# An encoder layer: where the first three weight slots of the projections are loaded and split

## The chip, the cores and the metric

The kernel runs on one core of one Trainium2 chip. The time is device microseconds of the whole program, from one execution to the next the median of several. The engines are PE (matrix products), PEld (PE's weight loads), DVE (vector), ACT (scalar), POOL (GpSimd) and SP, which issues all DMAs of this kernel.

## The reference

One layer of a hybrid encoder on two groups of 512 rows (here: prompt and sample), D = 1024, all in float32. Cut to what matters here:

```python
def _swiglu(x, w_gu, w_down):
    gate, up = jnp.split(x @ w_gu, 2, axis=-1)
    return (jax.nn.silu(gate) * up) @ w_down

def _layer(x, mem, p):
    x = _layernorm(ALPHA * x + 0.5 * _swiglu(x, p['ffn1_wgu'], p['ffn1_wd']), p['ln1_g'], p['ln1_b'])
    h = x @ p['w_in']
    br_a = _mla(h[..., :OFF_KV], h[..., OFF_KV:OFF_RWKV], ...) @ p['p_mla']
    br_b = _rwkv7(h[..., OFF_RWKV:OFF_GATE], ...) @ p['p_rwkv']
    gates = jax.nn.sigmoid(h[..., OFF_GATE:] + p['b_gate']).reshape(b, s, N_BRANCH, D_MODEL)
    mix = (gates[:, :, 0] * br_a + gates[:, :, 1] * br_b) @ p['w_o']
    x = _layernorm(ALPHA * x + mix, p['ln2_g'], p['ln2_b'])
    x = _layernorm(ALPHA * x + _cross(x, mem, ...), p['ln3_g'], p['ln3_b'])
    x = _layernorm(ALPHA * x + 0.5 * _swiglu(x, p['ffn2_wgu'], p['ffn2_wd']), p['ln4_g'], p['ln4_b'])
```

The change lies between the first `_layernorm` and `h = x @ w_in`.

## The kernel before

**Numbers in two parts.** Every float32 operand of a product is split into a high part (a rounding cast, ACT, line 246) and a low part (the operand minus its high part, a subtraction on DVE, line 180, or for x on POOL, line 247). A product is three matmuls: high times high, high times low, low times high (`Bank.prod`). In the profile `whl` is a weight slot's two parts, `wraw` the slot as loaded, `xh` and `xl` the parts of x, `ps` a PSUM bank.

**Weight slots.** A slot is 128 x 1024 numbers (512 KB). `Stream.fetch` takes a raw buffer and a split buffer, issues the load on SP, and writes the cast and the subtraction. The stream `st` feeds everything behind the first feed-forward block; of every four of its slots three use a pool with three split buffers and two raw ones, and the fourth a split buffer of its own with a raw one of that pool. The feed-forward block's weights (`FfnWeights`) use the same buffers, so slots 0 to 2 of `st` take over from the block's last weights.

**First feed-forward block.** `ffn` computes both groups together by Strassen's scheme with seven products (`strassen`), named "1" to "7". The down projection runs in 15 steps (`DOWN`, `down_step`); the last one has m = 3, four pairs, and takes the products in the order 1, 2, 6, 5, 3, 7, 4 (`AT_LAST`). The function `ahead` of a step is called before each of its seven products, with the product's place. Additions on DVE follow the products as their operands appear (`todo`).

**First LayerNorm.** When the last step's sums of a group are there, its x is transposed on PE into banks and DVE takes the statistics (`BlockNorm.add`, `BlockNorm.stats`); the shift `ln_h` is the last of them. Then eight tiles of x are normalised (`Norm.applying`): two DVE instructions, an activation on ACT, a cast on ACT and the low part on POOL. The first group's first three tiles are written ahead of the second group's statistics, the others behind them. `stats` with `hold` sets `k.after`: from then on every DVE instruction that the program writes gets an order behind that shift (class `Held`), until line 1041 sets `k.after = None`.

**Projections.** `compressed(2, "kv_norm_g", decay)` takes slots 0, 1 and 2 and multiplies them with x of one group, then the other, x tile by x tile over three banks at once (`abreast`); `compressed(3, "q_norm_g")` does so with slots 3, 4 and 5. Four banks carry the tag "a". A slot is fetched when the program asks for it:

```python
    def next_slot(self):
        while len(self.ready) <= self.ahead and self.n < len(self.slots):
            self.fetch()
        return self.ready.pop(0)
```

**What sets the order.** Each engine works its queue strictly as it was laid out beforehand. A planner lays it out: of the instructions whose inputs and buffers are there by its modelled times it takes the one that was written first in the program; orders written by hand (`order`, `Held`) are kept. So where a fetch is written decides how its cast and its subtraction rank among the others.

Of the kernel before, what the change touches and what calls it, by code (L numbers as in the profile page):

```python
# [42 lines left out]
def tiles_of(w, ns, ks):  # L43
# [40 lines left out]
DOWN = ((0, 0, 2), (1, 0, 2), (2, 0, 3), (3, 0, 3), (0, 2, 4), (1, 2, 5), (2, 3, 6), (3, 3, 6), (0, 4, 7), (1, 5, 8),  # L84
        (2, 6, 9), (0, 7, 10), (1, 8, 10), (2, 9, 10), (3, 6, 10))
# [219 lines left out]
def op_tiles(places):  # L305


    def pair(name):
        pool, tag, bufs = places[name]
        return [pool.tile([P, 4, T], F32R, name="xo", tag=tag, bufs=bufs) for _ in range(2)]  # L310

    return pair
# [214 lines left out]
            ra, rb = nxt  # L527


def ffn(k, fw, x32, std, rows_of, op_tile, posts, sums, d_h, d_s, norm_of, applied, last=False):  # L530

# [50 lines left out]
    def down_step(n, u2, u4):  # L584
        m, p0, p1_ = DOWN[n]

        def ahead(i):

            if i == 2 and m == 3:
                while due:  # L590
                    due.pop(0)()
            if i == 2:
                for p in range(p1_, max([p1_, *(b for _, _, b in DOWN[n + 1 : n + 2])])):
                    fetch(p)

        ps, done = {}, set()
        y = {(r, c): x32[:, rows_of[r], 2 * m + c] for r in range(2) for c in range(2)}

        def add(out, name, u):
            nc.vector.scalar_tensor_tensor(out=out, in0=ps[name].t, scalar=SC, in1=u, op0=ALU.mult, op1=ALU.add)  # L600

        final = n == len(DOWN) - 1

        def more(r, c, u):

            eng = nc.vector if final else nc.gpsimd
            eng.tensor_tensor(out=y[r, c], in0=y[r, c], in1=u, op=ALU.add)  # L607

        def to_y(r, c, name, u):
            add(y[r, c], name, y[r, c])  # L610
            if not final:
                more(r, c, u)

        def summed(i, x):

            x.add(m // 2)
            if m == 3 and not last:
                if i == 1:  # L620
                    going.append(applied(rows_of[0], norms[0]))
                    for _ in range(3):
                        next(going[0])
                BlockNorm.stats([x], True)
            elif m == 3 and i == 1:
                BlockNorm.stats(norms, True)

        todo = [
            ("p1", "1", lambda: nc.scalar.activation(out=u2, in_=ps["1"].t, func=AF.Identity, scale=SC)),
            ("c11", ("2", "p1"), lambda: to_y(0, 0, "2", u2)),  # L630
            ("u2", ("6", "c11"), lambda: add(u2, "6", u2)),
            ("u4", ("5", "u2"), lambda: add(u4, "5", u2)),
            ("u3", ("7", "u4"), lambda: add(u2, "7", u2)),
            ("c22", ("7", "u4"), lambda: to_y(1, 1, "7", u4)),
            ("c12", ("3", "u4"), lambda: to_y(0, 1, "3", u4)),
            ("c21", ("4", "u3"), lambda: to_y(1, 0, "4", u2)),
        ]
        if final:
            for name, (r, c, of, u) in {"d11": (0, 0, "p1", u2), "d12": (0, 1, "u4", u4), "d22": (1, 1, "u4", u4),
                                        "d21": (1, 0, "u3", u2)}.items():  # L640
                todo.insert(0, (name, (of,), lambda r=r, c=c, u=u: more(r, c, u)))
            todo = [(a, (*b, "d" + a[1:]) if a[0] == "c" else b, f) for a, b, f in todo]
        if p1_ == NP and m == 3:
            for r, x in enumerate(norms):
                todo.append((f"n{r}", (f"c{r + 1}1", f"c{r + 1}2"), lambda r=r, x=x: summed(r, x)))
        elif p1_ == NP and m == 1:
            due.extend(lambda r=r, x=x: summed(r, x) for r, x in enumerate(norms))
        strassen(k, fw, turn_of(n), ps, done, todo, p1_ - p0,
                 lambda o, i: tuple(slot(OPS.index(o), (p0 + i) % 4)[:, j] for j in range(2)), ahead)


    with posts() as sb:
# [13 lines left out]
        for g in range(G):  # L666
            xp = [std[g].pair(i) for i in range(KT)]
            banks = [Bank(k, "a") for _ in range(4)]
            ws = [[(o[0][:, i * P : i * P + P], o[1][:, i * P : i * P + P]) for i in range(KT)] for o in w]
            if last:  # L670
                abreast(banks, ws, xp)
            for j in range(2):
                pg, pu = banks[2 * j : 2 * j + 2]
                if not last:
                    for b, o in zip((pg, pu), ws[2 * j : 2 * j + 2]):
                        b.prod(b.t, list(zip(o, xp)))
                s = sb.tile([P, 2, T], F32, name="s", tag="s", bufs=2)[:, 0]
                nc.scalar.activation(out=s, in_=pg.t, func=AF.Silu)
                nc.vector.tensor_tensor(out=s, in0=s, in1=pu.t, op=ALU.mult)
                to_h(s, d_s[j][g], sb)  # L680
            if g == 0:
                for name in ("S1", "S2", "S3"):
                    ops[name] = op_tile(name)
                hold = [(0, slice(0, 2), sb.tile([P, 2, T], F32, name="up", tag="up", bufs=1))]
                for i in range(2):
                    t = sb.tile([P, 1, T], F32, name=("p1", "u4")[i], tag=("p1", "u4")[i], bufs=1)
                    hold.append((2, slice(i, i + 1), t))
                for name, a, b, op in (("S1", "A21", "A22", ALU.add), ("S2", None, "A11", ALU.subtract)):
                    for h in hold:
                        sums_of(name, a, b, op, *h)  # L690
# [112 lines left out]
def kernel(  # L803
# [15 lines left out]
    k = Ctx()  # L819
# [4 lines left out]
    def pool(name, side="left", space=None):  # L824
        kw = {} if space is None else {"space": space}
        return tc.tile_pool(name=name, bufs=1, side=side, reuse_waits="tile", **kw)
# [20 lines left out]
    d_h = [scratch(f"d_h_{p}", [P, 7, 2, T]) for p in range(NP)]  # L847
    d_s = [[scratch(f"d_s_{j}_{g}", [P, 2, T]) for g in range(G)] for j in range(2)]
# [46 lines left out]
    st = Stream(nc, plan, nc.vector)  # L895
    st.use(*[(wp, 3, 2)] * 3, (wide, 1, 0))
    k.ps = ctx.enter_context(pool("banks", space=PSUM))
    with ExitStack() as f1:
        fp, xo = f1.enter_context(pool("f1")), f1.enter_context(pool("xo"))
        fw = FfnWeights(k, wf1, [(wp, 3)] * 3 + [(wide, 1)], [(wp, 2)] * 2 + [(wide, 1)], wide)  # L900
        x32 = fp.tile([P, G, KT, T], F32, name="x32")
        xs = []
        for g in range(G):

            a = Acts(xpools[g], "x", 4, KT, "x")
            fw.ahead(1)
            for n in range(KT):
                if g == 0 and n < 2:
                    nc.sync.dma_start(out=x32[:, g, n], in_=x_t[:, g, n])
                elif n % 2 == 0:  # L910
                    nc.sync.dma_start(out=x32[:, g, n : n + 2], in_=x_t[:, g, n : n + 2])
                split(nc, a.hi(n), a.lo(n), x32[:, g, n])
                if (g, n) in ((0, 3), (1, 0)):
                    fw.ahead(1)
            xs.append(a)
        nc.sync.dma_start(out=cc, in_=cst)
        x1, ln = [], []

        def sums1():
            ln.append(f1.enter_context(pool("ln1")))  # L920
            return ln[0]

        def norm1(g):
            return BlockNorm(k, ln[0], lambda n: x32[:, g, n], "ln1_g", "ln1_b", ("c", "bc"[g]))

        def applied1(g, norm):
            def store(m):
                if m % 2:
                    nc.sync.dma_start(out=d_x1[g][:, m - 1 : m + 1], in_=x32[:, g, m - 1 : m + 1])

            if not x1:
                x1.extend(Acts(xpools[i], "x", 4, KT, "x") for i in range(G))
            return norm.applying(x1[g], store)

        places = {n: (xpools[0], "x", 4) for n in ("A11", "A12")}
        places.update({n: (xpools[1], "x", 4) for n in ("A22", "S4")}, **{n: (xo, "xo", 6) for n in ("S1", "S2", "S3")})
        ffn(k, fw, x32, xs, (0, 1), op_tiles(places), lambda: pool("post1"), sums1, d_h, d_s, norm1, applied1)

    def gate_out(n, g, h, t):
        nc.scalar.activation(out=t, in_=h, func=AF.Tanh, scale=0.5, bias=hbg[:, n : n + 1])  # L940
# [5 lines left out]
    with pool("p2") as sb:  # L946
# [172 lines left out]
        with pool("mla") as sm:  # L1119
# [8 lines left out]
            for h in range(HP):  # L1128
# [3 lines left out]
                for g in range(G):  # L1132
# [10 lines left out]
                    m = sb.tile([P, 8], F32, name="kkn", tag="kkn", bufs=2)  # L1143
# [161 lines left out]
    y32 = keep.tile([P, G, KT, T], F32, name="x32")  # L1305
# [147 lines left out]

    places = {n: (mixed, "xs", 8) for n in ("A11", "A12", "A22", "S4")}
    places.update({n: (keep, "xs", 4) for n in ("S1", "S2")}, S3=(of, "xo", 2))
    ffn(k, fw, y32, x3, (1, 0), op_tiles(places), lambda: pool("post2"), sums2, d_h, d_s, norm4, applied4, True)


def softmax(k, sb, s, scale):
# [544 lines left out]
```

## Time and profile before

| | |
|---|---|
| time, median of 3 runs (lowest, highest) | 2775.86 us (2774.26, 2776.49) |
| profiled execution, its own time | 2775.84 us |
| span of the profiled execution | 2774.1 us |
| granted PE clock, mean over the span | 0.963 |
| PE, PEld busy | 2605.6, 2079.9 us |
| DVE, ACT, POOL busy | 2123.8, 1095.9, 699.1 us |

All single times are microseconds from the start of the span. A row of a timeline gives start, length, engine, line, operation, output<-inputs, shape and count, and in brackets the engine's idle time before it and what ended it. A row of the chain of waits gives start, length and piece. The matmul of a 128 x 128 by 128 x 512 tile has a length of about 0.39 us in such rows; they overlap, and the time from one to the next is read from a stretch and its count.

### The profile page before, as it was taken

The numbers are of one execution on the slowest core, as the hardware profiler recorded it, in microseconds if no ns is written. First come the engines' busy times: TensorE is split into PE (matmuls) and PEld (weight loads), VectorE is DVE, ScalarE is ACT, GpSimd is POOL, SyncE is SP. The second block draws the span as 40 slices with busy tenths as digits, with TensorE's granted clock in tenths as the row PEclk, the third lists the DMA queues.
The fourth block names the chain that finished last, engine by engine and source line by source line (L and its number), as shares of the span: only waits on it lengthen the run. The fifth ranks groups of instructions, "written<-read, shape, count | busy, mean of one in ns | idle before, by whom it ended". The sixth has DMA issues, their size and how long they took to land.

```text
span 2774.1 us, 41500 instructions
## 1 busy us (share of the span) xinstructions
PE 2605.6 (94%) x15600; PEld 2079.9 (75%) x15600; DVE 2123.8 (77%) x3749; ACT 1095.9 (40%) x2008; POOL 699.1 (25%) x479
## 2 busy tenths in 40 slices
PE   8999999997899999997989888899999999999996
PEld 7888887785767777776777676677777888887784
DVE  7888887999366777758475768656798888887987
ACT  5334342223353555444443432224554343342222
POOL 0323332443100001133133321103032332332443
PEclk9999999999989999998899898999999999999998
DMA  4344437661244333343434354441101433447751
GB/s 171 130 150 160 152 145 296 235 235 57 95 165 150 112 106 111 111 143 129 131 109 131 119 178 126 161 174 42 54 31 67 161 144 138 152 162 267 273 202 68
DMA packets 164776, 398.18 MB, mean 144 GB/s; under 512 B 41120, under 2 KB 47520, under 8 KB 164576
## 3 DMA queue, kind: packets, MB, share of 16 engines
q1 hardware_dynamic: 164576, 395.53, 40.8%
q8 instruction: 124, 2.03, 0.3%
q14 instruction: 76, 0.62, 0.1%
HBM read 261.50 MB, written 133.96 MB: 143 GB/s over the span
## 4 chain that ended last, share of the span: by engine, by line
PE 76%; DVE 15%; ACT 3%; issue 2%; DMA 2%; POOL 1%; SPq 0%; POOLq 0%; ACTq 0%; DVEq 0%
PE ps L216 73%; PE ps L221 3%; DVE whl L180 2%; DVE dw L180 2%; DVE z L180 1%; DVE x L180 1%; DVE tm L180 1%; DVE rs L180 1%; DVE wt L180 1%; DVE s L180 1%; DVE ln_s L180 1%; DVE phi L180 1%; ACT whl L246 0%; DMA ld<-d_rw 0%; DVE up L180 0%
## 5 line engine op out<-in xcount | busy, mean ns | idle before, releaser
L216 PE MATMUL ps<-xh,whl 128*128 128x512 f32 x2688 | 890.2, 402 | 26.7 <-DVE whl L180 16.8
L216 PE MATMUL ps<-xo,whl 128*128 128x512 f32 x3792 | 899.7, 396 | 14.2 <-DVE z L180 8.5
L216 PEld LDWEIGHTS ps<-xo,whl 128*128 128x128 f32 x3792 | 713.0, 189 | 185.6 <-DVE z L180 6.7
L216 PEld LDWEIGHTS ps<-xh,whl 128*128 128x128 f32 x2688 | 507.8, 190 | 144.2 <-DVE whl L180 20.4
L216 PE MATMUL ps<-xl,whl 128*128 128x512 f32 x1344 | 535.1, 399 | 1.5 <-POOL xl L247 1.5
L180 DVE TENSOR_TENSOR whl<-wraw,whl 128x512 fp32r<-128x512 f32 (+4 forms) x273 | 282.5, 1045 | 63.6 <-ACT whl L246 62.9
L246 ACT CAST whl<-wraw 128x512 fp32r<-128x512 f32 (+4 forms) x318 | 223.9, 715 | 250.1 <-PE ps L216 210.8
L216 PEld LDWEIGHTS ps<-xl,whl 128*128 128x128 f32 x1344 | 255.8, 190 | 55.8 <-POOL xl L247 2.3
L709 POOL TENSOR_TENSOR s<-s,up 128x512 f32<-128x512 f32 x80 | 115.9, 1449 | 626.6 <-DVE up L180 391.1
L246 ACT CAST whl<-wt 128x512 fp32r<-128x512 f32 (+3 forms) x280 | 148.5, 555 | 276.0 <-PE ps L216 164.1
L180 DVE TENSOR_TENSOR whl<-wt,whl 128x512 fp32r<-128x512 f32 (+3 forms) x280 | 216.7, 795 | 10.8 <-ACT whl L246 10.3
L247 POOL TENSOR_TENSOR whl<-wraw,whl 128x1024 fp32r<-128x1024 f32 x45 | 109.1, 2426 | 385.5 <-ACT whl L246 355.4
L246 ACT CAST hop<-s 128x512 fp32r<-128x512 f32 x128 | 79.5, 621 | 238.2 <-POOL s L709 178.0
L180 DVE TENSOR_TENSOR hop<-s,hop 128x512 fp32r<-128x512 f32 x128 | 121.4, 949 | 55.4 <-ACT hop L246 48.0
L180 DVE SCALAR_TENSOR_TENSOR x<-ps,x 128x512 f32<-128x512 f32 x184 | 124.5, 683 | 50.6 <-PE ps L216 50.2
L180 DVE TENSOR_TENSOR wt<-wraw 128x512 f32<-128x512 f32 (+3 forms) x140 | 110.6, 791 | 1.0
L180 DVE TENSOR_TENSOR wt<-wraw,wt 128x512 f32<-128x512 f32 (+3 forms) x140 | 103.1, 737 | 4.2 <-DMA wraw<-in_wf_dram 2.1
L607 POOL TENSOR_TENSOR x<-x,s 128x512 f32<-128x512 f32 x48 | 70.7, 1478 | 129.4 <-DVE x L180 129.4
L247 POOL TENSOR_TENSOR xl<-x,xh 128x512 fp32r<-128x512 f32 x48 | 68.6, 1453 | 91.8 <-ACT xh L246 91.5
L180 DVE TENSOR_TENSOR p<-ps,p 128x512 f32<-128x512 f32 x120 | 82.2, 685 | 7.8 <-PE ps L216 4.8
L607 POOL TENSOR_TENSOR x<-x,z 128x512 f32<-128x512 f32 x48 | 71.3, 1486 | 52.8 <-DVE x L180 49.2
L216 PE MATMUL ps<-mh,whl 128*128 128x512 f32 x256 | 82.2, 401 | 0.0
(328 smaller groups left out, 3728.2 us busy)
## 6 DMA issues: line engine op xcount, KB each, us to landing
d_h<-hop SPq DMA_DIRECT2D x140, 512.0 KB, 2.6
xo<-d_h SPq DMA_DIRECT2D x140, 512.0 KB, 7.2
wraw<-in_wf_dram SPq DMA_DIRECT2D x95, 512.0 KB, 3.4
wraw<-in_wa_dram SPq DMA_DIRECT2D x57, 512.0 KB, 3.5
wraw<-in_wb_dram SPq DMA_DIRECT2D x36, 512.0 KB, 3.4
wraw<-in_wf_dram SPq DMA_DIRECT2D x36, 384.0 KB, 3.9
ld<-d_rw SPq DMA_DIRECT2D x24, 512.0 KB, 4.7
d_gate<-t SPq DMA_DIRECT2D x32, 256.0 KB, 2.4
```

What stands on the lines that cost most here:

```text
L180: inst = f(*args, **kw)
L216: self.last = order(k.tc, k.nc.tensor.matmul(out, a, b, start=start, stop=stop), self.last)
L221: self.last = order(self.k.tc, self.k.nc.tensor.transpose(out, a, ident), self.last)
L246: nc.scalar.copy(hi, src)
L247: (low or nc.vector).tensor_tensor(out=lo, in0=src, in1=hi.bitcast(F32), op=ALU.subtract)
L607: eng.tensor_tensor(out=y[r, c], in0=y[r, c], in1=u, op=ALU.add)
L709: nc.gpsimd.tensor_tensor(out=s[:, i], in0=s[:, i], in1=up[:, i], op=ALU.mult)
```

## The change

`ffn` gets an argument `early` in place of `last`. The first block is called with a function that fetches three slots of `st`; the second without one, where `last` was true before. `down_step` calls it in the last step before its fifth product, "3". The other edits only replace `not last` by `early` and move the line that sets `final` up. `Stream` and `compressed` are as they were: `compressed` now finds three slots ready.

```diff
-def ffn(k, fw, x32, std, rows_of, op_tile, posts, sums, d_h, d_s, norm_of, applied, last=False):
+def ffn(k, fw, x32, std, rows_of, op_tile, posts, sums, d_h, d_s, norm_of, applied, early=None):
...
     def down_step(n, u2, u4):
         m, p0, p1_ = DOWN[n]
 
+        final = n == len(DOWN) - 1
+
         def ahead(i):
 
             if i == 2 and m == 3:
                 while due:
                     due.pop(0)()
+            if i == 4 and final and early:
+                early()
             if i == 2:
...
-            if m == 3 and not last:
+            if m == 3 and early:
...
-            if last:
+            if not early:
                 abreast(banks, ws, xp)
...
-        ffn(k, fw, x32, xs, (0, 1), op_tiles(places), lambda: pool("post1"), sums1, d_h, d_s, norm1, applied1)
+        ffn(k, fw, x32, xs, (0, 1), op_tiles(places), lambda: pool("post1"), sums1, d_h, d_s, norm1, applied1,
+            lambda: [st.fetch() for _ in range(3)])
...
-    ffn(k, fw, y32, x3, (1, 0), op_tiles(places), lambda: pool("post2"), sums2, d_h, d_s, norm4, applied4, True)
+    ffn(k, fw, y32, x3, (1, 0), op_tiles(places), lambda: pool("post2"), sums2, d_h, d_s, norm4, applied4)
```

More of the change, by code (lines that the diff above doesn't have):

```diff
@@ L600, in add @@
             nc.vector.scalar_tensor_tensor(out=out, in0=ps[name].t, scalar=SC, in1=u, op0=ALU.mult, op1=ALU.add)
-        final = n == len(DOWN) - 1
         def more(r, c, u):
@@ L673, in ffn @@
                 pg, pu = banks[2 * j : 2 * j + 2]
-                if not last:
+                if early:
                     for b, o in zip((pg, pu), ws[2 * j : 2 * j + 2]):
```

## The prediction

> **What bounds the kernel now.** I read the page first, then the chain of waits around the first LayerNorm, then busy time by stretch, then single rows. Page, engines and chain shares:
>
> ```profile
> PE 2605.6 (94%) x15600; PEld 2079.9 (75%) x15600; DVE 2123.8 (77%) x3749; ACT 1095.9 (40%) x2008; POOL 699.1 (25%) x479
> PE 76%; DVE 15%; ACT 3%; issue 2%; DMA 2%; POOL 1%; SPq 0%; POOLq 0%; ACTq 0%; DVEq 0%
> ```
>
> PE sets the end nearly everywhere, so what counts is where PE stands idle. The diff touches the seam between the first feed-forward block and the projections. Busy time by stretch there (columns: PE, PEld, DVE, ACT, POOL busy with counts, granted PE clock, DMA share, GB/s):
>
> ```profile
> 655.00:673.00 18.00, 17.81 (x101) 14.49 (x99) 15.38 (x38) 1.05 (x1) 0.00 (x0) 1.00 0.01 2
> 673.00:684.40 11.40, 3.71 (x21) 2.26 (x19) 10.95 (x29) 4.20 (x6) 3.83 (x3) 0.83 0.12 47
> 684.40:700.70 16.30, 1.94 (x8) 1.57 (x8) 16.30 (x28) 14.37 (x24) 12.27 (x10) 0.50 0.42 172
> 700.70:707.65 6.95, 6.26 (x18) 3.95 (x18) 4.06 (x3) 2.94 (x4) 6.45 (x6) 0.74 0.84 279
> 707.65:768.60 60.95, 60.95 (x268) 50.15 (x269) 12.38 (x16) 16.92 (x27) 0.00 (x0) 1.00 0.16 52
> ```
>
> From 655 to 673 PE and DVE both work. From 684.4 to 700.7 PE does eight small transposes and DVE is full: PE waits for DVE. From 707.65 on PE runs without a gap. The chain of waits says for what (start, length, piece):
>
> ```profile
> 684.34 0.17 DVE ln_h L180
> ...
> 699.45 1.22 DVE whl L180
> 700.68 3.92 DMA wraw<-in_wa_dram
> 704.61 0.02 issue
> 704.63 1.06 ACT whl L246
> 705.69 0.02 issue
> 705.72 1.89 DVE whl L180
> 707.61 0.04 issue
> 707.65 59.75 PE ps L216 x261
> ```
>
> Call the three slots 0, 1, 2; each has a load (SP), a high part (a cast on ACT) and a low part (a subtraction on DVE, line 180). Slot 0's low part stands on DVE at 699.4, after the normalising multiplies and adds. Only when it is done does its raw buffer come free, so slot 2's load, cast and subtraction follow one after the other until 707.65. The waits and the single rows of SP, ACT and DVE agree:
>
> ```profile
> PE ps L216 <- DVE whl L180: 14.8, 2, 14.3
> ```
>
> ```profile
> 638.07 14.53 SPq L142 DMA_DIRECT2D wraw<-in_wa_dram  x2
> 700.68 0.33 SPq L142 DMA_DIRECT2D wraw<-in_wa_dram  x1
> ```
>
> ```profile
> 652.82 1.04 ACT L246 CAST whl<-wraw 128x1024 fp32r<-128x1024 f32 x1
> 661.82 1.05 ACT L246 CAST whl<-wraw 128x1024 fp32r<-128x1024 f32 x1 [7.96 <-PE ps L216]
> ```
>
> ```profile
> 699.37 1.29 DVE L180 TENSOR_TENSOR whl<-wraw,whl 128x1024 fp32r<-128x1024 f32 x1
> 701.18 1.70 DVE L180 TENSOR_TENSOR whl<-wraw,whl 128x1024 fp32r<-128x1024 f32 x1
> 705.72 1.88 DVE L180 TENSOR_TENSOR whl<-wraw,whl 128x1024 fp32r<-128x1024 f32 x1 [2.84 <-ACT whl L246]
> 736.09 1.23 DVE L180 TENSOR_TENSOR whl<-wraw,whl 128x1024 fp32r<-128x1024 f32 x1 [11.43 <-ACT whl L246]
> ```
>
> Slots 0 and 1 are loaded and cast by 662.9 already; only their low parts are late. The code says why: while `k.after` is set, every DVE instruction written after it stays behind the last norm's shift (684.34), and these subtractions rank behind the applies, which come first in program order.
>
> **What is removed and moved.** No instruction is added: three loads, three casts, three subtractions are written 30 to 50 us sooner, before the product "3" of the last down step and so before `k.after` is set. What can run when, and what it runs beside:
>
> Loads: slots 0 and 1 go out as now. Slot 2's needs slot 0's raw buffer; with the low part near 655 it goes out by about 656 and lands 3.92 later (chain row), near 660, where the DMA share is 0.01. On SP nothing else goes out from 652.6 until the first store of x, so nothing queues behind it:
>
> ```profile
> 679.37 0.33 SPq L929 DMA_DIRECT2D d_x<-x  x1
> ```
>
> Cost 0. If the cover were gone it would cost those 3.92.
>
> Casts: the low-part slots rotate through three buffers. Slot 2's buffer is the one that product "4" reads, the step's last. On PE, ACT and POOL (single rows):
>
> ```profile
> 672.00 1.17 PE L216 MATMUL ps<-xo,whl 128*128 128x512 f32 x4
> ```
>
> ```profile
> 687.75 1.12 ACT L246 CAST xh<-x 128x512 fp32r<-128x512 f32 x2
> ```
>
> ```profile
> 676.46 1.27 POOL L247 TENSOR_TENSOR xl<-x,xh 128x512 fp32r<-128x512 f32 x1 [23.11 <-ACT xh L246]
> 680.07 2.64 POOL L247 TENSOR_TENSOR xl<-x,xh 128x512 fp32r<-128x512 f32 x2 [2.34 <-ACT xh L246]
> 688.43 18.08 POOL L247 TENSOR_TENSOR xl<-x,xh 128x512 fp32r<-128x512 f32 x13 [5.72 <-ACT xh L246]
> ```
>
> So slot 2's cast starts at 673.2 and ends at 674.2 (1.05), while ACT is idle (1.05 busy of 18.0 up to 673). Cost 0 on ACT; behind it on ACT wait the norm's first activation and cast, whose result POOL takes up at 676.46.
>
> **The ceiling.** What is late next is x itself. Its tiles 0 to 2 of the first group are split by 682.7 (680.07 + 2.64); tile 3 comes at 688.43 + 18.08/13 = 689.8, after the second norm's shift at 684.34. Products per tile: 3 slots x 3 = 9 matmuls, 9 x 60.95/268 = 2.05 us, more than POOL's 1.39 per tile, so from tile 3 on PE is not starved. The two groups of slots 0 to 2 have 144 matmuls and the next three slots 144 more; before, these 288 end at 768.6. After: 27 are done with tiles 0 to 2, three of tile 3 need only its high part (688.4), so the remaining 261 start in effect at 689.1 and take 261 x 0.2274 = 59.4, to 748.5. Ceiling: 768.6 - 748.5 = 20.1 us.
>
> **What comes off it.** (a) The three subtractions now share DVE with the norms' statistics. DVE has 18.00 - 15.38 = 2.62 us idle from 655 to 673, room for two of 1.23, but not always where they fall; slot 2's falls where DVE is full (10.95 of 11.40) and everything behind it, the second norm's statistics above all, moves. Least: 1.2 (slot 2's alone). Most: 1.23 + 1.23 + 1.88 = 4.3. I take half of the first two and 1.3, 2.5. (b) Clock. PE ran at half clock after its rest (stretches):
>
> ```profile
> 684.40:686.50 2.10, 1.94 (x8) 1.57 (x8) 2.10 (x5) 0.17 (x1) 0.00 (x0) 0.50 0.00 0
> 700.70:702.00 1.30, 1.29 (x3) 1.10 (x4) 1.30 (x2) 1.10 (x2) 1.30 (x2) 0.50 0.97 309
> 702.00:703.00 1.00, 0.85 (x3) 0.13 (x2) 0.88 (x1) 0.79 (x2) 1.00 (x1) 0.50 0.81 283
> 703.00:704.00 1.00, 1.00 (x3) 0.81 (x4) 0.00 (x0) 0.00 (x0) 1.00 (x2) 0.50 0.94 373
> 704.00:705.00 1.00, 1.00 (x5) 0.83 (x4) 0.00 (x0) 0.37 (x1) 1.00 (x2) 0.84 0.94 266
> ```
>
> 3.3 us at 0.50 lose 1.65. Whether PE cools between tile 2 and tile 3 (684.8 to 688.4, with transposes in it) no row shows. Least 0. Most: cold from tile 1 on; a cold matmul takes 1.29/3 = 0.43, nine of them after 682.7 end at 686.6, which holds the second norm's transposes back by 2.2, plus 1.65: 3.9. I take 1.0, nearer to one half-paid warm-up. (c) Banks. Four are tagged "a", each group uses three, so the second group needs ACT to copy the first's out while ACT is 14.37 of 16.30 busy with applies. Least 0 (24 matmuls fit the free bank), most 2.4 (a copy behind three instructions of ACT's, at that stretch's mean of 14.37/24 = 0.6 each). I take 0.7, about one instruction.
>
> The Trainium skill, "TensorE: Matmul & The Clock Gate", Part 1, says that an idle window of about 3.4 us halves the clock and a busy one of as much restores it. The rows agree in the restoring (0.50 up to 704.0, 0.84 in the next us). It speaks against the change: by it the wait for tile 3 alone may cool PE, (b) would be 1.7 and the gain 15.2, against 16.9 with no cooling at all.
>
> Sum: 20.1 - 2.5 - 1.0 - 0.7 = 15.9 us; best 18.9, worst 9.5. The sum is made against the profiled execution's 2775.84 (span 2774.1 and 1.7 around it), 0.02 from the median 2775.86. Forecast 2759.9, say **2760.0**; its own range is 2756.9 to 2766.3. The rest of the kernel should move with it: after 768.6 the loads and splits wait for PE's buffers.
>
> **Rivals.**
>
> First, the planner puts slot 2's subtraction on DVE ahead of the first norm's statistics. It can't end before 673.2 + 1.05 + 1.23 = 675.5; the statistics' tail stood at 668.75, so all of it moves by 6.7 and (a) is 6.7 + 1.2 = 7.9 instead of 2.5. Gain 10.5: 2765.3. For it: these subtractions now rank ahead of everything written after product "3". Against: the planner places an instruction when it deems it ready.
>
> ```profile
> 668.75 0.17 DVE L180 TENSOR_SCALAR ln_v<-ln_m 128x4 f32<-128x4 f32 x1
> ```
>
> Second, no change, 2775.8: the low parts stay behind the norm, or a fixed wait after 768.6 takes the gain. Against the former, `k.after` is None when they are written; against the latter, I find no wait there that isn't counted from PE's own progress.
>
> Third, the slower side: the planner orders the remaining 2005 us anew, and splits of later slots fall behind runs of DVE work as slot 0's did. The waits of PE after 768.6, and the stretch:
>
> ```profile
> PE ps L216 <- DVE whl L180: 4.1, 3, 2.0
> ```
>
> ```profile
> 768.60:2774.10 2005.50, 1876.77 (x12425) 1488.23 (x12423) 1503.33 (x2862) 816.71 (x1510) 472.64 (x321) 0.96 0.40 135
> ```
>
> Its place is slots 3 to 7, whose splits DVE does between 708 and 771. Price of one such stall 14.3, as measured; two cost 28.6 - 15.9 = 12.7: 2788.5. It decides once PE's waits for low parts after the seam grow by more than 15.9. Against it: there they are 4.1 in all, and `k.after` is reset as before.
>
> **Chances.** Forecast 0.76, first rival 0.10, no change 0.06, slower 0.08. A measurement here can tell 0.2% (5.5 us). Faster 0.86, same 0.06, slower 0.08. The range is 2755 to 2768: the forecast's own, two microseconds more on either side for the first rival and for a replanned remainder.
>
> **What would show it.** Right: PE's 14.3 us wait for whl gone; slot 2's load issued before 660; its low part near 675; nine matmuls per tile for tiles 0 to 2 before 687; a gapless PE run from about 691 to 695; the second norm's shift at 685.5 to 689. Wrong: a shift later than 690 (step a), PE at 0.50 beyond the first 4 us of that run (b), PE waiting for ACT's copies between the groups (c), or a seam shorter by 15 with an unchanged total, which would mean that the rest was ordered worse.

## The result, and the profile after

The changed kernel takes **2759.93 us** (median of 4 runs, 2758.81 to 2765.2) against 2776.18 for the kernel before on the same chip (4 runs, 2774.26 to 2776.51). The ratio is 0.9947, 95% interval 0.9929 to 0.9964. The forecast was 2760.0. The profiled execution is the slowest of the four: own time 2765.2, span 2763.4.

The page of the changed kernel, engines and chain shares:

```profile
PE 2608.0 (94%) x15600; PEld 2082.7 (75%) x15600; DVE 2123.3 (77%) x3749; ACT 1094.4 (40%) x2008; POOL 697.9 (25%) x479
PE 55%; DVE 12%; ACT 3%; issue 2%; DMA 2%; POOL 1%; SPq 0%; POOLq 0%; ACTq 0%; DVEq 0%
```

The chain reaches back only to 705 us in this profile, so its shares don't add up to the whole and are not to be set against the 76% of before. Counts of instructions and busy times are those of before within 0.2%; the gain is idle time of PE, and it lies in the seam. Busy time by stretch (columns as in the prediction):

```profile
655.00:673.00 18.00, 17.84 (x98) 14.29 (x96) 16.61 (x37) 3.46 (x4) 0.00 (x0) 1.00 0.28 88
673.00:684.40 11.40, 7.61 (x36) 5.68 (x36) 11.26 (x24) 4.93 (x7) 2.24 (x2) 0.85 0.22 78
684.40:700.70 16.30, 13.51 (x60) 10.11 (x60) 15.92 (x34) 11.12 (x19) 10.33 (x9) 1.00 0.35 139
700.70:707.65 6.95, 6.83 (x30) 5.18 (x29) 4.34 (x6) 6.51 (x12) 6.95 (x6) 1.00 0.65 246
707.65:768.60 60.95, 57.48 (x247) 46.34 (x247) 23.41 (x52) 21.62 (x35) 2.34 (x4) 0.91 0.22 73
```

PE's 1.94 us of work between 684.4 and 700.7 have become 13.51, at full clock. The wait that is gone, from PE's rows of the kernel before:

```profile
700.71 1.22 PE L216 MATMUL ps<-xh,whl 128*128 128x512 f32 x2 [14.32 <-DVE whl L180]
...
707.65 0.73 PE L216 MATMUL ps<-xh,whl 128*128 128x512 f32 x2 [0.48 <-DVE whl L180]
```

It was ended by slot 0's low part, the subtraction that ran from 699.37 to 700.66; slot 2's, done at 707.6, ended a wait of 0.48. DVE's rows in the changed kernel show the low parts of slots 0, 1 and 2 and the two shifts:

```profile
660.02 1.20 DVE L180 TENSOR_TENSOR whl<-wraw,whl 128x1024 fp32r<-128x1024 f32 x1
...
664.20 1.23 DVE L180 TENSOR_TENSOR whl<-wraw,whl 128x1024 fp32r<-128x1024 f32 x1
...
673.36 0.16 DVE L180 SCALAR_TENSOR_TENSOR ln_h<-ln_m,ln_v 128x4 f32<-128x4 f32 x1
...
674.64 1.21 DVE L180 TENSOR_TENSOR whl<-wraw,whl 128x1024 fp32r<-128x1024 f32 x1
...
687.91 0.16 DVE L180 SCALAR_TENSOR_TENSOR ln_h<-ln_m,ln_v 128x4 f32<-128x4 f32 x1
...
702.93 1.51 DVE L180 TENSOR_TENSOR whl<-wraw,whl 128x1024 fp32r<-128x1024 f32 x1
```

All three stand ahead of the second shift (687.91) instead of behind the applies; the row at 702.93 is now slot 3's. What PE does with it, from its own rows:

```profile
686.06 0.61 PE L216 MATMUL ps<-xh,whl 128*128 128x512 f32 x2
688.02 0.62 PE L221 MATMUL ps<-cc,ln_v 128*128 128x128 f32 x4 [1.34 <-DVE ln_v L180]
...
691.98 0.96 PE L216 MATMUL ps<-xh,whl 128*128 128x512 f32 x3 [1.03 <-ACT xh L246]
693.35 0.50 PE L216 MATMUL ps<-xl,whl 128*128 128x512 f32 x1 [0.41 <-POOL xl L247]
...
704.14 0.62 PE L216 MATMUL ps<-xh,whl 128*128 128x512 f32 x2
704.59 0.39 PE L216 MATMUL ps<-xl,whl 128*128 128x512 f32 x1
704.82 0.62 PE L216 MATMUL ps<-xh,whl 128*128 128x512 f32 x2
...
708.16 0.50 PE L216 MATMUL ps<-xl,whl 128*128 128x512 f32 x1 [0.28 <-POOL xl L247]
```

It waits for x (`xh`, `xl`) here, no longer for a slot: 1.03 for the high part of tile 3 at 691.98 and 0.41 for its low part at 693.35, then it runs, with short stops at 706.91 and 708.16.

**How runs are compared below.** Profiles are laid over one another at the same matmul, counted from the start of the kernel. Every later profile, of whatever kernel, is already 0.8 to 2.8 us behind the profile of before at matmul 2500, where PE's order is still the same in all of them; this offset (1.34 in the changed kernel) is taken off. The *seam* is then how much sooner the last of the 288 products ends than the 768.6 of before: **16.7 us** in the changed kernel, against 15.9 predicted. Of the kernel before there is one profile, so a chance share in its own 768.6 would be in every seam alike. The *shift* is the start of the second norm's `ln_h`, offset taken off: 687.91 - 1.34 = 686.6, against 684.34 before.

The profiled execution has a span only 10.7 us shorter than before's, because it loses some 9 us again between 1590 and 1930, where the instructions stand in the same order as before. A second profile of the same kernel (below) loses 0.3 there, and its span is 17.3 shorter than before's, so this belongs to the execution. It isn't the changed kernel's alone: e9_behind loses 6.6 in the same place, e4_double 6.3, e6_last 5.6, the others 0.9 to 3.5. What it is was not settled.

### The profile page after: what moved, and what is told of

The parts are those of the page before. It is cut to its first block, busy times and chain, and to the rows that moved or that the text cites. A ratio compares the mean times of both kernels' runs of the same rounds, so it can differ in the third digit from the quotient of the medians.

```text
span 2763.4 us, 41505 instructions
## 1 busy us (share of the span) xinstructions
PE 2608.0 (94%) x15600; PEld 2082.7 (75%) x15600; DVE 2123.3 (77%) x3749; ACT 1094.4 (40%) x2008; POOL 697.9 (25%) x479
## 4 chain that ended last, share of the span: by engine, by line
PE 55%; DVE 12%; ACT 3%; issue 2%; DMA 2%; POOL 1%; SPq 0%; POOLq 0%; ACTq 0%; DVEq 0%
PE ps L216 52%; PE ps L221 3%; DVE dw L180 2%; DVE whl L180 1%; DVE tm L180 1%; DVE z L180 1%; DVE x L180 1%; DVE phi L180 1%; DVE ln_s L180 1%; DVE rs L180 1%; ACT whl L246 0%; DMA ld<-d_rw 0%; POOL ln_z L358 0%; DVE bk L180 0%; DVE wt L180 0%
```

## The experiments

Ratios are to the kernel before, run alongside on the same chip. The runs are from several chips, so the medians themselves are not to be set against each other.

| run | median us | ratio, 95% interval | shift | seam |
|---|---|---|---|---|
| changed kernel | 2759.93 | 0.9947 (0.9929 to 0.9964) | 686.6 | 16.7 |
| e0_again | 2759.99 | 0.9933 (0.9921 to 0.9946) | 686.7 | 16.6 |
| e1_unheld | 2764.55 | 0.9944 (0.9923 to 0.9965) | 688.0 | 16.3 |
| e2_two | 2764.21 | 0.9948 (0.9932 to 0.9965) | 685.6 | 13.9 |
| e3_pool | 2762.07 | 0.9936 (0.9920 to 0.9952) | 686.0 | 17.2 |
| e4_double | 2766.73 | 0.9957 (0.9941 to 0.9973) | 690.0 | 9.7 |
| e5_four | 2761.29 | 0.9940 (0.9928 to 0.9953) | 687.8 | 15.5 |
| e6_last | 2767.14 | 0.9955 (0.9940 to 0.9969) | 688.3 | 12.9 |
| e7_mixed | 2761.64 | 0.9940 (0.9927 to 0.9952) | 687.8 | 15.4 |
| e8_last_behind | 2763.44 | 0.9937 (0.9925 to 0.9949) | 688.4 | 14.9 |
| e9_behind | 2760.93 | 0.9928 (0.9916 to 0.9940) | 686.6 | 16.7 |

All intervals overlap that of the changed kernel: in time no run is told from it. The seam and the rows do the telling.

### The order behind the shift, or the place of the fetch?

The kernel before, with the stream's DVE instructions freed of the order behind the shift; the fetch stays where it was:

```diff
-    st = Stream(nc, plan, nc.vector)
+    st = Stream(nc, plan, tc.nc.vector)
```

> The three slots are fetched where the kernel before fetches them, behind the block and its norm; only the subtractions of the stream are freed of the order behind the norm's shift. Theory (the order behind the shift is what made PE wait; the place in the program matters only as a rank): the planner fills DVE's gaps with the low parts of slots 0 and 1 near 660 to 665, slot 2's follows its cast before or within the second norm's statistics; PE's 14.3 us wait for low parts is gone, time 2758 to 2763. Rival (the rank is what counts: freed but written last, they still come after the applies): PE still waits some 10 us or more for low parts, time 2768 to 2776.

Seam 16.3: nearly the whole gain without moving a fetch. DVE of this run (its line 247 is the subtraction, no longer wrapped):

```profile
660.30 1.20 DVE L247 TENSOR_TENSOR whl<-wraw,whl 128x1024 fp32r<-128x1024 f32 x1
...
664.46 1.23 DVE L247 TENSOR_TENSOR whl<-wraw,whl 128x1024 fp32r<-128x1024 f32 x1
...
671.92 1.22 DVE L247 TENSOR_TENSOR whl<-wraw,whl 128x1024 fp32r<-128x1024 f32 x1
...
684.06 1.17 DVE L247 TENSOR_TENSOR whl<-wraw,whl 128x1024 fp32r<-128x1024 f32 x1
```

The planner fills them in at 660 to 684 by itself, slot 3's too (671.92; slot 2's is the one at 684.06). The theory holds: the wait that PE had was made by the written order, not by the planner's rank. What the place of the fetch decides is which low parts come ahead of the shift.

### Does slot 2 matter?

```diff
-            lambda: [st.fetch() for _ in range(3)])
+            lambda: [st.fetch() for _ in range(2)])
```

> Only slots 0 and 1 are fetched early, slot 2 stays behind the norm. Its load is no longer late (slot 0's raw buffer is free by 662), only its low part is, at about 704. Theory: PE takes the products of all three slots x tile by x tile in its queue, so the first product that needs slot 2's low part stops it until about 705; against the changed kernel, where PE starts near 692, it loses 5 to 12 us: 2765 to 2772. Rival (the chain of load, cast and subtraction of slot 2 after 700.7, 7 us, was the smaller part and two thirds of the products are free of slot 2, so PE works on these): the loss is under 3 us, 2760 to 2763.

The seam loses 2.8 us, so the rival holds, although slot 2's low part still stands among the applies: done at 704.68, offset taken off 702.1, against 707.6 before. DVE of this run, slot 2's and slot 3's:

```profile
703.20 1.48 DVE L180 TENSOR_TENSOR whl<-wraw,whl 128x1024 fp32r<-128x1024 f32 x1
...
705.20 1.69 DVE L180 TENSOR_TENSOR whl<-wraw,whl 128x1024 fp32r<-128x1024 f32 x1
```

PE never stood still for slot 2 (between 684 and 760 its waits are for `xh`, `xl` and the second norm alone): it multiplied with slots 0 and 1 meanwhile, and slot 2's products came behind them. The 14.3 us of before were the wait for the first of the three slots, since all of them stood at the end of the applies or behind. So the prediction's chain, in which slot 2's load, cast and subtraction follow one after the other until 707.65, was the end of the critical path and not what the wait cost.

The 2.8 are a balance. When tile 3's high part came, PE had 268 of the 288 products left instead of 261 (1.6 us). Stops from there on cost 4.1 instead of 1.9: PE was at half clock from 692.28 to 695.70, after a rest of 2.2, and waited longer for POOL, beside which two subtractions of DVE stood at the end of the applies. The shift, with one subtraction less ahead of it, came 1.0 sooner. 1.6 + 2.2 - 1.0 = 2.8.

### DVE time ahead of the second shift

Each of the three subtractions twice, with the same result (not shown: `twice` is a new argument of `fetch`, set for these three):

```diff
-        split(nc, hl[:, 0], hl[:, 1], raw, self.low)
+        split(nc, hl[:, 0], hl[:, 1], raw, self.low); twice and self.low.tensor_tensor(
+            out=hl[:, 1], in0=raw, in1=hl[:, 0].bitcast(F32), op=ALU.subtract)
```

> The three early subtractions are done twice each (same result), so DVE has 3.7 us more to do there. Theory (each microsecond of DVE work ahead of the second shift moves PE's start, but for DVE's idle time of about 1.3 us that is still left before 673): the shift comes 2.0 to 3.7 us later than in the changed kernel, time 2762 to 2764. Rival (hidden): within 1 us, 2759 to 2761.

3.6 us of added DVE work put the shift back by 3.4: next to nothing of it is hidden. The seam falls by 7.0, though, twice as much, and the median lies above the 2762 to 2764 of the theory. DVE, POOL and PE of this run show the rest:

```profile
706.91 5.29 DVE L180 TENSOR_TENSOR whl<-wraw,whl 128x1024 fp32r<-128x1024 f32 x1
712.13 0.68 DVE L180 TENSOR_TENSOR s<-s,ps 128x512 f32<-128x512 f32 x1
```

```profile
695.98 15.14 POOL L247 TENSOR_TENSOR xl<-x,xh 128x512 fp32r<-128x512 f32 x12 [5.71 <-ACT xh L246]
```

```profile
711.52 0.39 PE L216 MATMUL ps<-xh,whl 128*128 128x512 f32 x1
714.41 1.28 PE L216 MATMUL ps<-xh,whl 128*128 128x512 f32 x2 [2.51 <-ACT xh L246]
```

```profile
714.40:717.50 3.10, 3.09 (x7) 2.31 (x8) 0.00 (x0) 1.47 (x3) 1.29 (x1) 0.54 0.65 266
```

Slot 3's subtraction, 1.51 in the changed kernel, takes 5.29 here, beside twelve low parts of x that POOL does back to back (695.98 to 711.1). The last addition of the applies waits behind it on DVE until 712.13, the last tile of x is late, PE stands still after 711.52, and then works at half clock (0.54) for most of 3.1 us. Matmuls starting more than 0.2274 apart cost 4.7 us in the run of products here, 1.2 in the changed kernel. 3.4 + 4.7 - 1.2 = 6.9 of the 7.0.

The three fetches later, before the seventh product:

```diff
-            if i == 4 and final and early:
+            if i == 6 and final and early:
```

> All three fetches are written before the last product, "4", instead of before "3"; the subtractions of slots 0 and 1 then stand on DVE behind the first norm's shift, beside slot 2's. Theory (DVE between the first shift and the second is full, so what falls there is paid in full, and what falls before 673 about half): second shift 1 to 2 us later than in the changed kernel, the seam's gain 14.5 to 16 us. Rival (DVE's order doesn't matter at this size): the same to 0.5 us.

As expected the second shift is later. The first shift comes no later than in the changed kernel (673.31 - 2.10 = 671.2 against 673.36 - 1.34 = 672.0), the second 1.7 later: all three subtractions now stand between the two. But the seam, 12.9, is under the 14.5 to 16 of the theory. Slot 3's subtraction took 5.30 again (705.43), and 2.9 us passed between two matmuls from 710.05 on; the stops cost 3.2. 1.7 + 3.2 - 1.2 = 3.7 of the 3.8 by which the seam fell.

A fourth fetch:

```diff
-            lambda: [st.fetch() for _ in range(3)])
+            lambda: [st.fetch() for _ in range(4)])
```

> Four slots are fetched early; slot 3's subtraction leaves the end of the applies, where it stands beside POOL's, and stands in the first norm's statistics. Theory: the second shift comes 1.2 us later, for one subtraction more ahead of it, and the end of the first six slots 0.5 to 1.5 us later than in the changed kernel. Rival (slot 3's subtraction holds up the last x tile and the banks' copies): 0.5 to 2 us sooner.

Slot 3's subtraction, now among those ahead of the shift, puts it back by 1.2, and the seam falls by 1.2. Two other effects cancel. Nothing stands beside POOL's run any more (16.40 for thirteen tiles, 17.35 in the changed kernel), and PE's stops at the end of the applies, 0.95 in all, are gone. But PE did the last matmuls of tiles 0 to 2 at half clock, from 691.39 on, and so reached tile 3 only at 696.01, 5.8 us behind the shift instead of 4.1. Stretches of this run:

```profile
690.30:694.10 3.80, 3.79 (x15) 3.21 (x16) 3.80 (x8) 1.91 (x3) 0.00 (x0) 0.57 0.07 29
694.10:707.00 12.90, 12.90 (x58) 10.71 (x57) 11.90 (x20) 12.90 (x23) 12.71 (x11) 0.99 0.56 225
```

### The low parts on POOL

All three, and slot 2's alone (not shown: `fetch` hands its new argument to `split` as the engine of the subtraction):

```diff
-            lambda: [st.fetch() for _ in range(3)])
+            lambda: [st.fetch(nc.gpsimd) for _ in range(3)])                       # e3_pool
+            lambda: [st.fetch(low) for low in (None, None, nc.gpsimd)])           # e7_mixed
```

> The three early low parts are computed on POOL instead of DVE; POOL is idle from 654 to 680 and takes 2.43 us for each. Theory (what the change still pays is DVE time ahead of the second norm's shift, 2.2 us in the trace): the shift comes 2.0 to 2.5 us sooner than in the changed kernel and PE's gapless run with it, 2757 to 2758. Rival (DVE's price is hidden, x's own split or PE's clock sets the start): no difference, 2759 to 2761. Second rival (slot 2's low part on POOL, ready 676.7 at the earliest, holds up x's low parts behind it, and DVE's two-input instructions slow down beside POOL): slower, 2761 to 2764.

> Only slot 2's low part goes to POOL; PE's and DVE's order is otherwise that of the changed kernel. It runs from 674 to 677, when POOL is idle and DVE's instructions read PSUM. Theory (slot 2's subtraction, 1.2 us on a full DVE, is most of what the change pays): the second norm's shift and PE's run come 1.0 to 1.5 us sooner than in the changed kernel. Rival (x's first low part is held up on POOL behind it and takes the gain back): no difference in the time from the block's end to PE's run, or later.

With all three on POOL the shift is 0.6 sooner, not 2.0 to 2.5, and the seam 0.5 longer, for 3.6 us of work taken off DVE. With slot 2's alone the shift is 1.2 later and the seam 1.3 shorter, though DVE has an instruction fewer: both theories fell. POOL and DVE of e7_mixed:

```profile
675.64 2.35 POOL L247 TENSOR_TENSOR whl<-wraw,whl 128x1024 fp32r<-128x1024 f32 x1 [20.18 <-ACT whl L246]
```

```profile
675.94 2.59 DVE L180 TENSOR_TENSOR x<-x,z 128x512 f32<-128x512 f32 x1
```

The addition of two SBUF tiles that takes 0.68 in the changed kernel takes 2.59 here: it starts 0.30 behind POOL's instruction and ends 0.5 behind its end. In e3_pool the pair `x<-x,s`, 1.29 in the changed kernel, took 3.49 from 665.17, beside POOL's subtraction from 665.62 to 668.1. DVE pays in waiting what it no longer pays in work. The Trainium skill, "SBUF — State Buffer", section "Who interferes with whom", says that a DVE instruction with two SBUF inputs contends with a GpSimd instruction that reads SBUF, and that the port pair that they share is an exclusive lock; these rows agree.

In e7_mixed the wait is 1.9 us for 1.2 saved. The other half microsecond fits the clock, though no run separates it: PE transposes x for the second norm's statistics, and at half clock from 679.35 on two groups of these transposes took 1.11 and 1.97 us, against 0.66 and 1.59 in the changed kernel.

### Slot 3's subtraction at the end of the applies

One pair of neighbours on DVE swapped: slot 3's low part behind the last addition of the applies. Once on e6_last, once on the changed kernel (not shown: `split` returns its subtraction, and the additions of `ln_sh` are kept in the list `applies`):

```diff
-        split(nc, hl[:, 0], hl[:, 1], raw, self.low)
+        inst = split(nc, hl[:, 0], hl[:, 1], raw, self.low)
+        if self.n == 3:
+            order(k.tc, inst, applies[-1])   # the last apply's addition of ln_sh
```

> The variant in which the three fetches stand before the seventh product of the last down step, with one pair of neighbours on DVE swapped: slot 3's low part comes behind the last addition of the second group's applies, not ahead of it. In that variant slot 3's low part took 5.30 us from 705.43, beside POOL's twelve low parts of x back to back, the last x tile came late by it, and PE stood still for 2.9 us at 710.05. Theory (the subtraction, which reads two tiles of SBUF, waits for POOL and holds up the last addition behind it): the addition, which reads one operand from PSUM, goes through in 0.7 us, PE's gap of 2.9 falls under 0.6, and the end of the first 288 products comes 2.3 to 3.3 us sooner than in that variant, 15.2 to 16.2 us before the kernel before instead of 12.9; the low part itself may still take 5 us, and nothing waits for it. Rival (POOL's back-to-back run, or ACT behind it, is what is late, and the long subtraction only stands beside it): the gap stays at 2 us or more and the end moves by less than 1 us. Time about 2.9 us under that variant's, 2764 by its median of 2767.

The long stop is gone. DVE and PE of this run:

```profile
706.25 0.69 DVE L180 TENSOR_TENSOR s<-s,ps 128x512 f32<-128x512 f32 x1
706.86 2.08 DVE L180 TENSOR_TENSOR whl<-wraw,whl 128x1024 fp32r<-128x1024 f32 x1
```

```profile
709.39 0.61 PE L216 MATMUL ps<-xh,whl 128*128 128x512 f32 x2
710.14 0.50 PE L216 MATMUL ps<-xl,whl 128*128 128x512 f32 x1
710.48 0.64 PE L216 MATMUL ps<-xh,whl 128*128 128x512 f32 x2
711.39 0.50 PE L216 MATMUL ps<-xl,whl 128*128 128x512 f32 x1 [0.27 <-POOL xl L247]
```

The addition, with one input in PSUM, goes through in 0.69. PE's stops fall from 3.2 to 1.2 and the seam grows by 2.0, a little under the 2.3 that the theory gave at the least. So in e6_last the subtraction did hold up the last tile; in e4_double the rows are the same, but the swap was not run there.

> The changed kernel with the same swap: slot 3's low part behind the last addition of the applies. In the changed kernel that low part took 1.51 us and PE had gaps of about 1 us in all from 706.4 to 708.5, when the last x tiles came. Theory (those gaps are the wait for the last x tile behind slot 3's low part): they fall to 0.3 or less and the end of the 288 products comes 0.6 to 1.2 us sooner, 17.3 to 17.9 us before the kernel before instead of 16.7. Rival (the gaps are ACT's copies of the first group's banks): they stay, and the end moves by less than 0.4. The time, 2759 to 2760, can't tell the two apart from the changed kernel.

Here the theory fell: seam 16.7 and the short stops of 0.95 us as before the swap. The rival's numbers came true, but not its cause: in the changed kernel none of PE's waits between 690 and 752 is for a copy of ACT's. POOL's rows say what the stops are (the changed kernel, e9_behind, e1_unheld):

```profile
692.00 17.35 POOL L247 TENSOR_TENSOR xl<-x,xh 128x512 fp32r<-128x512 f32 x13 [5.92 <-ACT xh L246]
```

```profile
692.19 17.33 POOL L247 TENSOR_TENSOR xl<-x,xh 128x512 fp32r<-128x512 f32 x13 [5.92 <-ACT xh L246]
```

```profile
693.72 16.39 POOL L247 TENSOR_TENSOR xl<-x,xh 128x512 fp32r<-128x512 f32 x13 [6.12 <-ACT xh L246]
```

The first two runs of thirteen low parts are a good 0.9 longer than the third. In e1_unheld slot 3's subtraction stands at 671.92, and PE has no such stop at all, though it starts on tile 3 at the same distance behind POOL (1.35 us); e5_four, where the subtraction is gone from there too, has 16.40 and no stop. Ahead of the last addition or behind it, the subtraction takes its turn from POOL, and PE waits for POOL. PE catches up with POOL because it takes the tiles of the second group through the one free bank first: 0.68 per tile (rows 704.14 and 704.82 above) against 16.39 / 13 = 1.26.

### The same kernel again

The changed kernel as it is, for the spread of such a comparison:

> The changed kernel once more. In its profile it won 16.7 us at the seam and gave 6 of these back between 1590 and 1930, where the program's order is the same as before. Theory (that part is chance of the single execution, PE's clock falling to one half at other moments): the new profile has the same seam, PE's 288 products of the first six slots ending 16 to 17 us sooner than before, counted from the end of the block's products, and its span is below 2760 or differs elsewhere. Rival (a cost of the change): it gives back 5 us or more in the same place.

Shift 686.7, seam 16.6, span 2756.8. The theory holds: the loss between 1590 and 1930 is not there. Two profiles of one kernel agree in the seam to 0.15 us. e3_pool's seam alone is longer than the changed kernel's by more than that (0.5), and in time it can't be told from it.

## Why the prediction was right

- **The ceiling (20.1)** held: x is what is late next. Tile 3's low part begins at 692.00, PE follows at 693.35. With three matmuls already done, the run of 261 begins in effect at 693.35 - 0.68 - 1.34 = 691.3 and ends by 0.2274 each at 750.7; with the stops of 1.2 that makes 751.9, which is 768.6 - 16.7.
- **(a) DVE time, 2.5**: measured 2.2 (686.6 against 684.34), of which 0.9 is there at the first shift (672.0 against 671.1 in the row of before below). The bounds of 1.2 and 4.3 were fair; e4_double shows that work added on top, ahead of the second shift, is paid almost in full (3.4 of 3.6).

```profile
671.13 0.16 DVE L180 SCALAR_TENSOR_TENSOR ln_h<-ln_m,ln_v 128x4 f32<-128x4 f32 x1
```

- **(b) Clock, 1.0**: measured nothing in the changed kernel. PE was at half clock from 679.7 to 683.1, on matmuls of tiles 0 to 2 that it finished ahead of tile 3 anyway, and at 1.00 from 684.4 to 707.65. The wait for tile 3, which I had feared as 3.6 long and cooling, was 1.03. The term itself is real: e5_four lost about 0.9 by it (its seam's 1.2 = 1.2 of shift - 0.95 of stops + 0.9).
- **(c) Banks, 0.7**: the size was near, the cause wrong. No matmul of this run waited for a copy of ACT's; PE had enough to do in the free bank, which I had only as the lower bound. It lost 1.2, of which 0.95 to POOL's low parts, which the subtraction of slot 3 delays. I had taken POOL's 1.39 per tile to be faster than PE's 2.05 throughout; in the second group PE takes 0.68 per tile.
- **Slot 2's chain** as the price of the wait: the wrong end. The 14.3 us ended at 700.7 with slot 0's low part, and slot 2's left 0.48; with slots 0 and 1 early, holding slot 2 back cost 2.8 in e2_two. The sum doesn't rest on this reading, for it starts from the tiles of x.
- **Signs that came wrong without a cost**: slot 0's low part stood at 660.0, not near 655, slot 2's load went out at 661.25, not before 660 (its cast still began at 673.20, when product "4" was done), and the matmuls of tiles 0 to 2 were done by 691, not 687, since the second norm's transposes (688.02) went ahead of the last nine; all are ahead of tile 3.
- **First rival** (slot 2's subtraction ahead of the first norm's statistics): didn't occur; 674.64 lies behind the shift at 673.36. **No change**: the gain stayed. **Slower side**: PE's waits for low parts behind the seam are 5.7 against 4.1 before, where 15.9 more was its point:

```profile
PE ps L216 <- DVE whl L180: 5.7, 3, 2.8
```

The terms behind the ceiling, 4.2 by forecast, came to 3.4. Their split was partly luck: (b) too high by 1.0, (c) too low by 0.5.

## What to carry to other kernels

When a consumer waits for several inputs, look which of them ends the wait, and ask what it could do with the others: the input that ends the critical path need not be the one that made it wait. Work put into an engine whose chain sets the next release is hidden only as far as that engine is idle (three subtractions cost 2.2 of 3.6 us here, three more 3.4 of 3.6), and on DVE it also has a price in the turns that it takes from POOL, or loses to it. Before moving work to POOL look at which DVE instructions beside it read two SBUF tiles.

## What the runs showed of the hardware

**The clock is set by windows, and half a window of work mostly keeps it.** In all twelve profiles the granted clock changes only at a fixed grid of 3.41 us. Two pairs of neighbouring windows of that grid in the changed kernel and one in e5_four (stretches, columns as before: the second number after the window is PE's busy time, the third last the clock):

```profile
676.30:679.70 3.40, 1.42 (x10) 1.01 (x11) 3.40 (x7) 1.39 (x2) 0.00 (x0) 1.00 0.48 157
679.70:683.10 3.40, 3.20 (x10) 2.31 (x10) 3.40 (x8) 1.22 (x3) 1.27 (x1) 0.50 0.00 0
...
686.50:689.90 3.40, 2.06 (x14) 1.72 (x14) 3.13 (x12) 0.00 (x0) 0.00 (x0) 1.00 0.00 0
689.90:693.35 3.45, 2.01 (x8) 1.02 (x6) 3.45 (x6) 3.45 (x6) 1.35 (x2) 1.00 0.37 152
```

```profile
687.50:690.90 3.40, 1.74 (x10) 0.99 (x9) 3.19 (x9) 0.00 (x0) 1.87 (x2) 0.99 0.06 22
690.90:694.30 3.40, 3.40 (x12) 2.81 (x11) 3.40 (x7) 2.11 (x4) 0.01 (x1) 0.50 0.14 55
```

1.42 and 1.74 us of work in a window were followed by half clock, 2.06 by full clock, and no rest of PE's in them was longer than 2.8. Counted over all twelve profiles: of 138 windows at full clock with matmuls in under 40% of them, every one was followed by half clock; between 40% and 75%, 80 of 331; with 75% and more, 22 of 8527. Back from half clock it took a window nearly full: none of the 293 below 85%, 209 of the 282 above 95%. The Trainium skill, "TensorE: Matmul & The Clock Gate", Part 1, has these windows, free-running, and calls the one that cools idle; here it need not be idle. So a short rest costs nothing, or half of a window of 3.41 us that PE would have filled (1.7), by where it falls in the grid; e5_four's 0.9 and the half clock of e2_two may be of this kind.

**DVE can lose several turns to POOL.** The same subtraction, slot 3's at the end of the applies, took 1.51 us in the changed kernel (1.52 in three other runs), 2.08 and 2.04 with the swap (e8_last_behind, e9_behind), but 5.29 and 5.30 in e4_double and e6_last, beside the same kind of run of POOL's. In the short cases one of POOL's turns is longer (the thirteen take 17.35 instead of 16.39), in the long ones twelve go through at 1.26 each and DVE's ends only after them. If DVE had only to wait for the instruction that POOL was at, it would wait 1.3 at most; it waited for the rest of one and three more. What decides who gets the turn was not found: the subtraction had started 0.87 us after the POOL instruction beside it in the changed kernel and 0.86 after it in e6_last.

**POOL also stretches tiny instructions.** At the end of the second norm instructions of 128 x 4 numbers, 0.17 each when alone, take longer beside it. DVE of the changed kernel:

```profile
683.62 1.15 DVE L180 TENSOR_SCALAR rs<-ln_v 128x4 int32<-128x4 int32 x1
684.81 1.30 DVE L180 TENSOR_SCALAR rs<-rs 128x4 int32<-128x4 int32 x1
```

That is 2.1 us in the chain to the second shift, beside POOL's low parts of x tiles 1 and 2 (683.43 to 684.75 and 684.80 to 686.08), at whose ends the two also end. The kernel before has 1.9 there, the other runs 1.9 to 2.1: no run took it away.
